# Moving the state-space scan from VectorE to GpSimd in a hybrid layer, with a masked bias table and new room around the scan units

## The chip, the cores and the metric

The kernel runs on one core of a Trainium2 chip. The metric is the device time of one execution in microseconds (us); the kernel before takes 2429.09 us, the median of three runs between 2426.07 and 2430.97. In the profile PE is TensorE (matmul), PEld its weight loads, DVE is VectorE, ACT is ScalarE, POOL is GpSimd, and SP is SyncE, whose queue issues all DMAs of this kernel; SPq, PEq and so on are the sequencers that hand work to the engines.

## The reference

One layer of a streaming encoder over 2048 frames of 1024 features, in float32. One input projection feeds two groups of heads side by side; their outputs are normalised, joined and projected, and a gated feed-forward block follows.

```python
h = rmsnorm(x, norm_mix_g)
u, q, k, v = split(h @ w_in)                      # 512 columns each
# group A: state-space layer, 32 groups of 16 channels, 64 complex states each
lam_bar = exp(lam * dt)
b_bar = (lam_bar - 1) / lam * b
states[t] = lam_bar * states[t - 1] + b_bar @ u[t]
y = gelu(Re(c @ states) + d * u)
y_ssm = y * sigmoid(y @ w_glu + b_glu)
# group B: 8 heads of 64; a chunk of 64 frames attends to itself and the 8 chunks before it
scores = q @ k.T / 8 + bias[head, clip(rel, -128, 128)]   # outside the band: -1e30
y_att = softmax(scores) @ v
x = x + concat(rmsnorm(y_ssm), rmsnorm(y_att)) @ w_out
h2 = rmsnorm(x, norm_ffn_g)
x = x + (silu(h2 @ w_gate) * (h2 @ w_up)) @ w_down
return rmsnorm(x, norm_final_g)
```

## The kernel before

Every matmul operand is held as a high part, rounded for the matmul, and a low part, the rest; a product is three matmuls (`mm3`: high by high, high by low, low by high). High parts are copies on ACT, and the low part is one subtraction, `lo = x - hi`, on DVE or POOL.

**The stages.** From 0 to about 138 us the kernel projects `u`, the input of the state-space layer, in four blocks of 512 columns (`prep`, `group`, `finish`, lines 406 to 482). For each block, `prep` loads eight tiles `xt` (L417), copies their high parts (L419) and subtracts their low parts on DVE (L420); `group` runs 24 matmuls for each of four output tiles. Beside this, `ssm_prologue` builds the powers of `lam_bar` and the small matrices of the state-space layer on DVE (the generator `pro` is advanced between the blocks). Its largest part multiplies six products of 128x576 four times over (tiles `cm` and `v`, lines 273 to 280); these `v` are stored to a DRAM table `vs`. Then come the first transposed, normalised activations `hT`, and the first query, key and value projections; 128 attention steps follow, from 193 to about 832 us; then the gate of the state-space output and the output projection, the gate and up projections (to about 1950 us), and the down projection.

**The attention stage.** `att_phase` emits 128 steps. A step computes the scores of 128 queries of one head against 640 keys (`sc`), adds the bias tile `nb` and takes the minimum on DVE (L736), takes the exponential on ACT (L739), transposes (`pt`, then `pth` on ACT and `ptl` on DVE, L754 and L755), and after four steps multiplies by the values (`pj<-pth,v`). `units` are generators that add work between these parts: the projections of the next 512 frames, and the eight units of the state-space layer. Each `Unit` is advanced by a share of its yields at every step; the matmuls are kept in program order on PE, so the place of a yield fixes what stands in front of what. A state-space unit has `SSM_N` = 42 yields over 15 steps.

**One state-space unit** (`ssm_unit`, lines 486 to 571) serves four of the 32 groups. It loads `U` (8 DMAs), `Bst`, `Tm` and `Vm`, waits `YL` yields, projects with `pj<-U,Bst` (L508; ACT copies the result to `X`, L511), scans, copies the states in four DMAs to `XG` (L557, which also changes their layout), waits `YX` yields, and forms the output with `pj<-U,Tm` and `pj<-XG,Vm` (L565, L566); ACT copies it and eight DMAs store `y` (L570). All tiles of a unit come from a pool with one buffer for each name, and the output tile of a unit bears the name `X` as well. So the next unit's `U` can be loaded only when this unit's output matmuls have read theirs, and its `X` can be written only when the stores of `y` are done.

**The scan.** Along the 256 time blocks it works in groups of eight, with four instructions a step (`step`, lines 525 to 528: multiply, multiply by the swapped part, add, add): 7 steps on 128x128 elements, 7 on 128x16, 3 on 128x4. Two rounds of `carry` (L536, L537) then spread the ends: 8 instructions on 128x42 and 8 on 128x434. The 128 elements of a step stand every eighth in a row of `X`, so 32 bytes apart. In the kernel before these 84 instructions of each unit run on DVE.

**The bias tile.** At the first of a head's four steps `nb` is loaded from the DRAM table `nbs` (L715), and two memsets on POOL write 1e30 into its corners (L716, L717). The low parts of the activations (L640) and of the query, key and value weights (in `split`, L151) are on POOL, but for half of those of the first 512 frames. The split weights are stored to `wss` right behind their split (L613).

The line numbers of helpers stand for many callers: L74 is every matmul, L150 and L151 are the two parts of `split`.

Of the kernel before, what the change touches and what calls it, by code (L numbers as in the profile page):

```python
# [13 lines left out]
ALU = mybir.AluOpType  # L14
AX = mybir.AxisListType

P = 128
# [6 lines left out]
NC = SEQ // L  # L24
GB, GP = 4, 2
H, HD = 8, 64
SB = 512
NSB = SEQ // SB
# [23 lines left out]
CUTL = -8, -2, 2, 7, 13, 19, 23  # L52
ORDER = "sptf"
PINA = True
YL = 8
YX = 9
X1B = 6
TAIL = (0, 512), (512, 256), (768, 256)
MAGIC = 12582912.0
# [32 lines left out]
def f32(ap):  # L92
    return ap.bitcast(F32)
# [297 lines left out]
def u_phase(k, ident, S):  # L391

    tc, nc, io = k.tc, k.nc, k.io
    with ExitStack() as cx:
# [78 lines left out]
        for b in range(1, 4):  # L473
            prep(b)
            next(pro)
            now = [group(b, 0)]
            finish(b - 1, held)
            now += [group(b, 1), group(b, 2)]
            sums(b)
            held = now + [group(b, 3)]  # L480
# [5 lines left out]
def ssm_unit(k, p, psum, S, b, eng):  # L486

    nc = k.nc
# [60 lines left out]
    yield from carry(Xe[:, :, :, 1:, :7], Xe[:, :, :, :3, 7], 8, 3)  # L549
    yield from carry(Xk[:, :, :, 1:, :7], Xk[:, :, :, : NC // 8 - 1, 7], 0, NC // 8 - 1)  # L550

    XG = k.t(p, "XG", [P, GB, NC])
    XGv = XG[:].rearrange("p (q g) c -> p q g c", g=2)
    nc.gpsimd.memset(XG[:, :, 0:1], 0.0)
    for g2 in range(2):
        for c in range(2):
            nc.sync.dma_start(XGv[c * NS : (c + 1) * NS, :, g2, 1:], X[g2 * NS : (g2 + 1) * NS, c, :, : NC - 1])  # L557
# [13 lines left out]
        yield  # L571


SSM_N = YL + GP + 7 + 7 + 3 + 4 + YX + GP


class Unit:
# [21 lines left out]
def att_phase(k, ident, S, pro):  # L599
    tc, nc, io = k.tc, k.nc, k.io  # L600
    with ExitStack() as cx:
        aw = tc.alloc_tile_pool(name="aw", reuse_waits="tile", bufs=1, side="right")
        pfs = cx.enter_context(tc.tile_pool(name="apf", bufs=2, space=bass.MemoryType.PSUM, reuse_waits="tile"))
        hT, vts, qk = {}, {}, {}

        def load_w(sb, n):

            w = k.t(aw, "w", [P, 2, 1024], F32R, bufs=WB)
            if sb == 0:
                raw = k.t(aw, "raw", [P, 1024], bufs=2)  # L610
                nc.sync.dma_start(raw[:], io["w_qk"][n] if n < 8 else io["w_v"][n - 8])
                split(k, w[:, 0], w[:, 1], raw[:], k.wlo_eng)
                nc.sync.dma_start(S["ws"][n], f32(w[:]))  # L613
            else:
                nc.sync.dma_start(f32(w[:]), S["ws"][n])
            return w[:, 0], w[:, 1]

        def hT_unit(sb, q0=0, q1=KT):
            hi, lo = hT.setdefault(sb, ([], []))
            ts = slice(sb * SB, (sb + 1) * SB)  # L620
            xts = {}

            def load(q):
                if q < q1:
                    x = f"{('hi', 'lo')[q % 2]}{q // 2}x" if sb == 0 and q < 2 * DB else None
                    xts[q] = k.t(aw, x, [P, SB]) if x else k.t(aw, "xt", [P, SB], bufs=XB)
                    nc.sync.dma_start(xts[q][:], io["xt"][q * P : (q + 1) * P, ts])

            ahead = 2 if sb else KT
            for q in range(q0, q0 + ahead):  # L630
                load(q)
            for q in range(q0, q1):
                yield
                load(q + ahead)
                xt = xts[q]
                for v, n in zip(hT[sb], ("hi", "lo")):
                    v.append(k.t(aw, f"{n}{q}x" if q < DB and sb % 2 else f"{n}{q}", [P, SB], F32R))
                nc.vector.scalar_tensor_tensor(xt[:], xt[:], k.gm[:, q : q + 1], S["rsn"][:, ts], op0=ALU.mult, op1=ALU.mult)
                nc.scalar.copy(hi[q][:], xt[:])  # L639
                (nc.gpsimd if sb or q % 2 else nc.vector).tensor_tensor(lo[q][:], xt[:], f32(hi[q][:]), op=ALU.subtract)  # L640
            yield

        def qk_unit(sb, pr):
# [11 lines left out]
            for c in range(2):  # L655
                ps = k.t(pfs, "pf", [P, 512])
                wh, wl = ws[c]
                for q in range(KT):
                    cs = slice(q * P, (q + 1) * P)
                    mm3(k.ta, ps[:], wh[:, cs], wl[:, cs], hi[q][:], lo[q][:], q == 0, q == KT - 1)  # L660
                    if q < KT - 1:
                        yield
                for hh in range(2):
# [17 lines left out]
        def v_unit(sb, fh):  # L681
# [5 lines left out]
            for i in range(4):  # L687
                ps = k.t(pfs, "pf", [P, 256])
                ic = slice(i * P, (i + 1) * P)
                for q in range(KT):  # L690
# [4 lines left out]
                    k.ta.matmul(ps[:], lo[q][:, ic], wh, start=False, stop=q == KT - 1)  # L695
                    if q % 2 and q < KT - 1:
                        yield
                vt = vts[4 * sb + i, fh]
                pv3 = ps[:].rearrange("p (h d) -> p h d", h=4)
                nc.scalar.copy(vt[:, :, :HD], pv3)  # L700
# [5 lines left out]
        class Head:  # L706
            pass

        def scores(st):
            sb, pr, hh, qp = st  # L710
            h = 2 * pr + hh
            if qp == 0:
                hd = st_head[sb, h] = Head()
                hd.nb = k.t(aa, "nb", [P, 640], bufs=2)
                nc.sync.dma_start(hd.nb[:], bass.AP(S["nb"].tensor, S["nb"].offset + h * 768 + 1, [[1, P], [1, 640]]))  # L715
                nc.gpsimd.memset(hd.nb[0:64, 0:64], 1e30)  # L716
# [769 lines left out]
def block_kernel(tc, io, phases="pusamf"):  # L1486
    nc = tc.nc
    k = K(tc, io)
    k.ssm_eng, k.wlo_eng = nc.vector, nc.gpsimd
    with ExitStack() as cx:  # L1490
        dram = cx.enter_context(tc.tile_pool(name="dram", bufs=1, space=bass.MemoryType.DRAM))
        cp = cx.enter_context(tc.tile_pool(name="const", bufs=1))
# [2 lines left out]
        def pp():  # L1495
# [2 lines left out]
        S = {  # L1498
            "u": k.t(dram, "u", [DS, L, NC]), "y": k.t(dram, "y", [DS, L, NC]),
            "ya": k.t(dram, "ya_s", [NSB, DS, SB]), "x1": k.t(dram, "x1", [D, SEQ]),  # L1500
            "k": k.t(dram, "ks", [2, H, P, SB]), "nb": k.t(dram, "nbs", [H, 768]),
            "bst": k.t(dram, "bsts", [4, P, 8 * P]), "v": k.t(dram, "vs", [NPR, 2, 2, NS, 9 * CH]),
            "hc": k.t(dram, "hc", [2, 7, P, 4, 512]), "h": k.t(dram, "hs", [4, P, HALF]), "ws": k.t(dram, "wss", [12, P, 2, 1024]),
            "hq": k.t(dram, "hq", [2, F2, 7, P, 512]), "wc": k.t(dram, "wc", [F2, 7, P, 512]), "wt": k.t(dram, "wt", [4, P, HALF]),
# [81 lines left out]
```

## Time and profile before

| what | value |
|---|---|
| median of 3 runs | 2429.09 us |
| the profiled execution, its own time | 2425.27 us |
| its span in the profile | 2423.5 us |
| mean granted clock of TensorE | 0.964 |
| PE busy in the span | 92% |
| DVE, ACT, POOL busy | 69%, 41%, 38% |

The profiled execution's own time is 1.8 us above its span; the rest lies around it. Busy shares are means over stages with different limits, so the stages are read apart. "Idle before, releaser" tells how long an engine stood before a group of instructions and what ended that.

### The profile page before, as it was taken

The numbers are of one execution on the slowest core, as the hardware profiler recorded it, in microseconds if no ns is written. First come the engines' busy times: TensorE is split into PE (matmuls) and PEld (weight loads), VectorE is DVE, ScalarE is ACT, GpSimd is POOL, SyncE is SP. The second block draws the span as 40 slices with busy tenths as digits, with TensorE's granted clock in tenths as the row PEclk, the third lists the DMA queues.
The fourth block names the chain that finished last, engine by engine and source line by source line (L and its number), as shares of the span: only waits on it lengthen the run. The fifth ranks groups of instructions, "written<-read, shape, count | busy, mean of one in ns | idle before, by whom it ended". The sixth has DMA issues, their size and how long they took to land.

```text
span 2423.5 us, 30933 instructions
## 1 busy us (share of the span) xinstructions
PE 2224.6 (92%) x10744; PEld 1862.5 (77%) x10744; DVE 1665.3 (69%) x2943; ACT 1000.3 (41%) x1671; POOL 909.0 (38%) x613
## 2 busy tenths in 40 slices
PE   6876878899998799999999999899999989999996
PEld 5655767788787678877888888688888868888886
DVE  8965688777878675656676666867655456569676
ACT  4233544455544754234333334433333343345322
POOL 4321210010100043257555555755555554445542
PEclk8887999999999999999999999999999989999998
DMA  5655676566554353564455455645433277555551
GB/s 159 174 194 203 216 206 199 174 192 191 169 176 123 121 170 122 183 229 149 135 183 177 158 187 206 237 170 202 154 122 95 71 295 253 190 200 200 182 191 70
DMA packets 223132, 425.75 MB, mean 176 GB/s; under 512 B 30384, under 2 KB 70832, under 8 KB 215872
## 3 DMA queue, kind: packets, MB, share of 16 engines
q1 hardware_dynamic: 222976, 423.79, 53.6%
q8 instruction: 84, 1.38, 0.2%
q14 instruction: 72, 0.59, 0.1%
HBM read 283.97 MB, written 129.26 MB: 171 GB/s over the span
## 4 chain that ended last, share of the span: by engine, by line
PE 56%; DVE 2%; DMA 2%; POOL 1%; issue 1%; ACT 1%; SPq 0%; DVEq 0%; POOLq 0%; ACTq 0%
PE X L74 18%; PE ps L74 18%; PE Y L74 9%; PE big L74 6%; PE W L74 5%; DMA lo<-hc 1%; DVE lo L151 1%; POOL c L151 0%; POOL lo L151 0%; POOL sa L1005 0%; DMA hd<-wc 0%; POOL sa L1004 0%; DVE acc L1451 0%; DVE S L1253 0%; DVE g L1318 0%
## 5 line engine op out<-in xcount | busy, mean ns | idle before, releaser
L74 PE MATMUL X<-hi,c 128*128 128x512 f32 x1408 | 451.2, 391 | 7.9 <-POOL c L151 3.2
L74 PE MATMUL ps<-hd,hd 128*128 128x512 f32 (+1 forms) x1968 | 434.7, 383 | 8.0 <-DVE hd L151 4.6
L74 PEld LDWEIGHTS ps<-hd,hd 128*128 128x128 f32 x1968 | 361.3, 191 | 80.1 <-DVE hd L151 4.9
L151 POOL TENSOR_TENSOR c<-S,c 128x512 fp32r<-128x512 f32 x176 | 251.8, 1432 | 243.8 <-ACT c L150 239.8
L74 PEld LDWEIGHTS X<-hi,c 128*128 128x128 f32 x1408 | 265.1, 188 | 65.5 <-ACT u L1271 4.0
L74 PE MATMUL X<-lo,c 128*128 128x512 f32 x704 | 274.9, 390 | 0.0
L151 POOL TENSOR_TENSOR hd<-hd 128x1536 fp32r<-128x1536 f32 (+1 forms) x53 | 190.3, 3596 | 208.7 <-ACT hd L150 185.5
L150 ACT CAST hd<-hd 128x1536 fp32r<-128x1536 f32 (+1 forms) x106 | 147.4, 1392 | 227.1 <-DMA hd<-hq 155.3
L151 POOL TENSOR_TENSOR c<-raw,c 128x512 fp32r<-128x512 f32 x132 | 189.6, 1436 | 130.6 <-ACT c L150 105.5
L74 PE MATMUL Y<-hi,c 128*128 128x512 f32 x704 | 227.2, 393 | 11.3 <-DVE u L1275 11.3
L1399 DVE TENSOR_TENSOR acc<-acc,ps 128x512 f32<-128x512 f32 x196 | 129.2, 682 | 87.0 <-PE ps L74 84.4
L74 PE MATMUL pf<-hi,w 128*128 128x512 f32 x416 | 157.7, 428 | 10.5 <-ACT hi L639 10.5
L74 PEld LDWEIGHTS Y<-hi,c 128*128 128x128 f32 x704 | 133.5, 190 | 41.0 <-DVE u L1275 13.0
L74 PE MATMUL big<-m,woh 128*128 128x512 f32 x512 | 163.7, 402 | 0.2 <-DVE yr L941 0.2
L150 ACT CAST c<-S 128x512 fp32r<-128x512 f32 x176 | 109.3, 621 | 114.6 <-PE Y L74 57.8
L74 PEld LDWEIGHTS X<-lo,c 128*128 128x128 f32 x704 | 132.7, 188 | 27.3
L716 POOL MEMSET nb<- 64x64 f32 x32 | 4.6, 144 | 387.9 <-DMA nb<-nbs 246.0
L1271 ACT COPY u<-X 128x512 f32<-128x512 f32 x132 | 76.9, 584 | 176.4 <-PE X L74 176.4
L739 ACT ACTIVATE s<-s,mn 128x640 f32<-128x640 f32 (+4 forms) x128 | 97.9, 765 | 121.4 <-DVE mn L736 102.9
L150 ACT CAST c<-raw 128x512 fp32r<-128x512 f32 x132 | 82.1, 622 | 149.7 <-PE Y L74 82.3
L736 DVE CUSTOM_DVE_ANT_0 s<-sc,nb 128x640 f32<-128x640 f32 (+4 forms) x128 | 94.1, 735 | 70.5 <-PE sc L74 56.6
L151 DVE TENSOR_TENSOR hd<-hd 128x1536 fp32r<-128x1536 f32 (+1 forms) x53 | 113.4, 2141 | 35.7 <-ACT hd L150 35.6
(370 smaller groups left out, 4812.2 us busy)
## 6 DMA issues: line engine op xcount, KB each, us to landing
w<-wss SPq DMA_DIRECT2D x36, 1024.0 KB, 5.5
hq<-g SPq DMA_DIRECT2D x140, 256.0 KB, 2.1
hd<-hq SPq DMA_DIRECT2D x42, 768.0 KB, 4.5
hd<-wc SPq DMA_DIRECT2D x42, 768.0 KB, 6.0
raw<-in_w_gate SPq DMA_DIRECT2D x44, 512.0 KB, 3.8
raw<-in_w_up SPq DMA_DIRECT2D x44, 512.0 KB, 4.2
wc<-px SPq DMA_DIRECT2D x66, 256.0 KB, 2.9
wss<-w SPq DMA_DIRECT2D x12, 1024.0 KB, 4.4
```

Of the source, the lines that this page charges most:

```text
L74: return self.tc.keep_in_program_order(self.tc.nc.tensor.matmul(*a, **b))
L150: nc.scalar.copy(hi, raw)
L151: (lo_eng or nc.gpsimd).tensor_tensor(lo, raw, f32(hi), op=ALU.subtract)
L716: nc.gpsimd.memset(hd.nb[0:64, 0:64], 1e30)
L736: nc.vector.tensor_tensor_reduce(s[:, :nk].rearrange("p (a b) -> p a b", a=nch), ps[:, :nch, :half], hd.nb[:, nk - 1 :: -1].rearrange("p ( ...
L739: nc.scalar.activation(s[:, :nk], s[:, :nk], AF.Exp, bias=mn[:], scale=-1.0, accum_out=sums[sb, pr][:, hh, qp : qp + 1])
L1271: nc.scalar.copy(u[:], ps[:])
L1399: V.tensor_tensor(a, a, ps[:], op=ALU.add)
```

## The change

The state-space scan goes to POOL (`k.ssm_eng`). The low parts of the attention weights, and of all activations but half of the first 512 frames', go to DVE (`k.wlo_eng`, and the choice at L640). A unit now waits 4 yields instead of 8 between its loads and its projection, 6 new yields stand between the end of the scan and the transfers to `XG`, and 7 instead of 9 behind those; the sum stays 42. `XG` is allocated once and its first column cleared once. The bias tiles with their corners are built once in a DRAM table `nbms`, with one DMA that expands 8x768 entries into 1024 rows of 640 (2.6 MB) and two that write the corners from a memset tile; a head's tile is loaded two steps before the head begins, and nothing is written into it. The stores of the split weights move behind the first matmuls that use them.

```diff
-YL = 8
-YX = 9
+YL = 4
+YW = 6
+YX = 7
...
         for b in range(1, 4):
             prep(b)
             next(pro)
+            if b == 2:
+                corner = k.t(p1, "corner", [64, H, 64])
+                nc.gpsimd.memset(corner[:], 1e30)
+                nc.sync.dma_start(S["nbm"][:], bass.AP(S["nb"].tensor, S["nb"].offset + 1, [[768, H], [1, P], [1, 640]]))
+                for m in range(2):
+                    nc.sync.dma_start(S["nbm"][:, m * 64 : m * 64 + 64, m * 576 : m * 576 + 64].rearrange("h p c -> p h c"), corner[:])
...
-    XG = k.t(p, "XG", [P, GB, NC])
+    if b == 0:
+        k.XG = k.t(p, "XG", [P, GB, NC])
+        nc.gpsimd.memset(k.XG[:, :, 0:1], 0.0)
+    XG = k.XG
     XGv = XG[:].rearrange("p (q g) c -> p q g c", g=2)
-    nc.gpsimd.memset(XG[:, :, 0:1], 0.0)
+    for _ in range(YW):
+        yield
...
                 split(k, w[:, 0], w[:, 1], raw[:], k.wlo_eng)
-                nc.sync.dma_start(S["ws"][n], f32(w[:]))
+                keep[n] = w
...
+        def keep_w(n):
+            if n in keep:
+                nc.sync.dma_start(S["ws"][n], f32(keep.pop(n)[:]))
...
-                (nc.gpsimd if sb or q % 2 else nc.vector).tensor_tensor(lo[q][:], xt[:], f32(hi[q][:]), op=ALU.subtract)
+                (nc.vector if sb or q % 2 == 0 else nc.gpsimd).tensor_tensor(lo[q][:], xt[:], f32(hi[q][:]), op=ALU.subtract)
...
+                    if q == 2:
+                        keep_w(4 * c + pr)
...
+                if i == 0:
+                    for r in range(2):
+                        keep_w(8 + 2 * r + fh)
...
+        def load_nb(h):
+            nb = k.t(aa, "nb", [P, 640], bufs=2)
+            nc.sync.dma_start(nb[:], S["nbm"][h])
+            return nb
...
-                hd.nb = k.t(aa, "nb", [P, 640], bufs=2)
-                nc.sync.dma_start(hd.nb[:], bass.AP(S["nb"].tensor, S["nb"].offset + h * 768 + 1, [[1, P], [1, 640]]))
-                nc.gpsimd.memset(hd.nb[0:64, 0:64], 1e30)
-                nc.gpsimd.memset(hd.nb[64:128, 576:640], 1e30)
+                hd.nb = nbs.pop(h) if nbs else load_nb(h)
...
+            if qp == 2 and (sb, h) < (NSB - 1, H - 1):
+                nbs[(h + 1) % H] = load_nb((h + 1) % H)
...
-    k.ssm_eng, k.wlo_eng = nc.vector, nc.gpsimd
+    k.ssm_eng, k.wlo_eng = nc.gpsimd, nc.vector
```

The order in which the instructions stand on an engine is set by the program and by a scheduler, and the change moves rows at two places that the prediction speaks of.

**SP in the projection of `u`, second block.** The rows run from the fourth `xt` of the block on. Before, `kts` is a table of the state-space layer, and the other four `xt` follow at once:

```order
L417 DMA xt_782<-in_xp 128x512
L363 DMA kts_79<-kt_1331 16x8x128
L417 DMA xt_791<-in_xp 128x512
L417 DMA xt_800<-in_xp 128x512
L417 DMA xt_809<-in_xp 128x512
```

Now the same place reads as below; `nbms` is the expansion of the bias table, `bbs` and `vs` are stores of what DVE has computed in the prologue (a second store of the same `bbs` pair and the rest of the first `vs` pair are left out at the lines of dots):

```order
L418 DMA xt_783<-in_xp 128x512
L480 DMA nbms_69<-nbs_70 1024x1x640
L344 DMA bbs_79<-bbr_563 64x16x16
L344 DMA bbs_79<-bbi_564 64x16x16
...
L352 DMA vs_72<-v_236_702 64x4x144
L352 DMA vs_72<-v_237_703 64x4x144
...
L352 DMA vs_72<-v_242_718 64x4x144
L352 DMA vs_72<-v_243_719 64x4x144
...
L418 DMA xt_792<-in_xp 128x512
L418 DMA xt_801<-in_xp 128x512
```

The last four `xt` loads of the block stand behind four stores of `bbs` and eight of `vs`.

**DVE at the same place.** These are the rows around the fifth and sixth low part of that block (`lo<-xt_791`, `lo<-xt_800`). Before, they stand among the powers of `lam_bar` (`pr`, `pi`):

```order
L282 TENSOR_TENSOR bbi_563<-cm_193_569,cm_194_570 128x256
L420 TENSOR_TENSOR lo_270_794<-xt_791,hi_269_793 128x512
L273 TENSOR_TENSOR cm_197_580<-pr_574 128x16
L274 TENSOR_TENSOR cm_198_581<-pi_575 128x16
L420 TENSOR_TENSOR lo_274_803<-xt_800,hi_273_802 128x512
L275 TENSOR_TENSOR pr_574<-cm_197_580,cm_198_581 128x16
```

Now they stand behind all powers and behind 23 of the 24 multiplications of 128x576 that form `v`:

```order
L279 TENSOR_TENSOR cm_340_1059<-pi_576,ci_340 128x576
L276 TENSOR_TENSOR v_337_1056<-cm_339_1058,cm_340_1059 128x576
L278 TENSOR_TENSOR cm_341_1063<-pr_575,ci_340 128x576
L279 TENSOR_TENSOR cm_342_1064<-pi_576,cr_339 128x576
L421 TENSOR_TENSOR lo_271_795<-xt_792,hi_270_794 128x512
L421 TENSOR_TENSOR lo_275_804<-xt_801,hi_274_803 128x512
L281 SCALAR_TENSOR_TENSOR v_338_1057<-cm_341_1063,cm_342_1064 128x576
```

What moved is the second half of the block's low parts: 160 rows of DVE stood ahead of them, now 253 do.

**PE between two state-space units.** Behind the first unit's output the rows are the same up to the last `pf<-w,lo` below; `sc`, `pj<-ident,rb` and `pt` belong to the attention step that follows, `pf<-hi,w` to the next projection. Before:

```order
L74 MATMUL pf_2702<-w_2431,lo_467_1593 128x256
L74 MATMUL sc_2796<-k_593_2217,q2h_2215 128x512
L74 MATMUL sc_2796<-k_593_2217,q2l_2216 128x512
L74 MATMUL pj_2803<-ident_80,rb_2758 128x128 x4
L77 MATMUL pt_2810<-ident_80,s_2681 128x128 x2
L74 MATMUL pf_2823<-hi_452_1557,w_2715 128x512
```

Now:

```order
L75 MATMUL pf_2698<-w_2456,lo_469_1597 128x256
L75 MATMUL pj_2793<-U_2721,Bst_2730 128x256 x2
L75 MATMUL pj_2800<-U_2721,Bst_2730 128x256 x2
L75 MATMUL sc_2813<-k_604_2243,q2h_2241 128x512
L75 MATMUL sc_2813<-k_604_2243,q2l_2242 128x512
L75 MATMUL pj_2820<-ident_81,rb_2754 128x128 x4
```

The projection `pj<-U,Bst` of the next unit stands sixteen rows sooner behind the output of the unit before it; the output matmuls of the units have kept their places.

More of the change, by code (lines that the diff above doesn't have):

```diff
@@ L571, in ssm_unit @@
         yield
-SSM_N = YL + GP + 7 + 7 + 3 + 4 + YX + GP
+SSM_N = YL + GP + 7 + 7 + 3 + 4 + YW + YX + GP
 class Unit:
@@ L603, in att_phase @@
         pfs = cx.enter_context(tc.tile_pool(name="apf", bufs=2, space=bass.MemoryType.PSUM, reuse_waits="tile"))
-        hT, vts, qk = {}, {}, {}
+        hT, vts, qk, keep = {}, {}, {}, {}
         def load_w(sb, n):
@@ L707, in att_phase @@
             pass
+        nbs = {}
+        def load_nb(h):
+            nb = k.t(aa, "nb", [P, 640], bufs=2)
+            nc.sync.dma_start(nb[:], S["nbm"][h])
+            return nb
         def scores(st):
@@ L1500, in block_kernel @@
             "ya": k.t(dram, "ya_s", [NSB, DS, SB]), "x1": k.t(dram, "x1", [D, SEQ]),
-            "k": k.t(dram, "ks", [2, H, P, SB]), "nb": k.t(dram, "nbs", [H, 768]),
+            "k": k.t(dram, "ks", [2, H, P, SB]), "nbm": k.t(dram, "nbms", [H, P, 640]), "nb": k.t(dram, "nbs", [H, 768]),
             "bst": k.t(dram, "bsts", [4, P, 8 * P]), "v": k.t(dram, "vs", [NPR, 2, 2, NS, 9 * CH]),
```

## The prediction

> **What bounds the kernel now.** I read the page first, then the windows of 60 us, then the waits of the attention stage, then the two ends of a state-space unit in the timeline.
>
> ```profile
> PE 2224.6 (92%) x10744; PEld 1862.5 (77%) x10744; DVE 1665.3 (69%) x2943; ACT 1000.3 (41%) x1671; POOL 909.0 (38%) x613
> PE   6876878899998799999999999899999989999996
> DVE  8965688777878675656676666867655456569676
> 0.00:60.00 60.00, 40.78 (x154) 32.00 (x155) 50.61 (x191) 28.12 (x48) 24.84 (x22) 0.86 0.59 159
> 60.00:120.00 60.00, 48.72 (x205) 39.29 (x204) 59.52 (x131) 15.96 (x28) 19.31 (x14) 0.89 0.61 173
> 360.00:420.00 60.00, 51.79 (x303) 44.53 (x304) 49.30 (x141) 28.98 (x59) 0.58 (x4) 1.00 0.63 184
> 213.45:795.20 581.75, 504.96 (x2994) 443.40 (x2993) 449.55 (x1219) 292.13 (x618) 55.66 (x97) 0.96 0.61 184
> ```
>
> The columns of a window are its length, the busy time of PE, PEld, DVE, ACT and POOL, and the granted clock. PE is nearly full from about 800 us on, and the change leaves the order of PE there alone: what is won or lost comes from the first 800 us. Of those, 60 to 120 us belong to DVE (59.52 of 60). In the attention stage PE leads but isn't full, and POOL is almost idle (0.58 of 60).
>
> ```profile
> DVE s L736 <- PE sc L74: 56.6, 31, 7.7
> PE pt L77 <- DVE ptl L755: 33.0, 32, 2.3
> PE sc L74 <- DVE mn L736: 23.2, 9, 10.5
> PE pj L74 <- DMA Tm<-kts: 11.2, 4, 3.7
> POOL nb L716 <- DMA nb<-nbs: 246.0, 21, 25.5
> ```
>
> These rows give the time waited in all, the times, and the longest. PE waits for DVE (33.0 and 23.2 us) where the scan delays `ptl` and `mn`, and four times for the loads of a unit (11.2). POOL's 246.0 us only show an idle engine.
>
> ```profile
> L74 PE MATMUL pj<-U,Bst x64: 377/379/634, 213.5 to 741.8; 128*128 128x256 f32 x64
> L74 PE MATMUL pj<-XG,Vm x64: 378/379/379, 275.1 to 795.2; 128*128 128x256 f32 x64
> 257.22 0.63 PE L74 MATMUL pf<-lo,w 128*128 128x512 f32 x1
> 257.65 1.05 PE L74 MATMUL pf<-hi,w 128*128 128x512 f32 x2
> 261.30 0.39 PE L74 MATMUL pf<-lo,w 128*128 128x512 f32 x1
> 261.53 0.62 PE L74 MATMUL pf<-hi,w 128*128 128x512 f32 x2
> ```
>
> The eight units reach from 213.45 (first `U,Bst`) to 795.2 (last `XG,Vm`): 582 us. A 128x512 matmul takes 0.23 us from start to start at full clock (261.30 to 261.53). With every form counted at its closest spacing, read in the same way (0.118 for 256 columns, 0.147 for a score of 320, 0.108 for a transpose, 0.216 for one of a unit's own), the PE work in these 582 us is 470 us, so **112 us are lost**; the window agrees, with 77 idle and a clock of 0.96. Behind a pause PE is slower for some 4 us (257.22 to 257.65: 0.43 a matmul), so a pause costs about 1.9 us more.
>
> **The scan's price on POOL.** First what it costs DVE, then POOL's rows.
>
> ```profile
> L525 DVE TENSOR_TENSOR st<-X,a x136: 163/182/2255, 217.6 to 770.5; 128x128 f32<-128x128 f32 x56, 128x16 f32<-128x16 f32 x56, 128x4 f32<-128x4 f32 x24
> L536 DVE TENSOR_TENSOR fx<-X,a x64: 153/596/2691, 239.1 to 781.2; 128x42 f32<-128x42 f32 x32, 128x434 f32<-128x434 f32 x32
> L525 DVE TENSOR_TENSOR st<-X,a 128x128 f32<-128x128 f32 (+2 forms) x136 | 40.9, 301 | 11.2 <-ACT X L511 8.0
> L537 DVE TENSOR_TENSOR X<-X,fx 128x42 f32<-128x42 f32 (+1 forms) x64 | 29.9, 468 | 1.0
> L1434 POOL TENSOR_TENSOR sb<-sb,sg x6: 724/736/746, 2387.4 to 2407.1; 128x256 f32<-128x256 f32 x6
> L151 POOL TENSOR_TENSOR c<-S,c x176: 1283/1292/1842, 1093.9 to 1937.1; 128x512 fp32r<-128x512 f32 x176
> 59.36 4.07 POOL L425 TENSOR_TENSOR acc<-acc,sq 128x512 f32<-128x512 f32 x3 [7.92 <-ACT sq L423]
> L527 DVE TENSOR_TENSOR X<-X,st 128x128 f32<-128x128 f32 x56 | 22.5, 402 | 0.0
> L755 DVE TENSOR_TENSOR ptl<-pt,pth 128x128 fp32r<-128x128 f32 x36 | 10.3, 286 | 2.8 <-ACT pth L754 2.4
> ```
>
> The six scan lines together take 214.5 us of DVE, 26.8 a unit. On POOL, 256 elements take 0.736 us and 512 take 1.292: 2.17 ns an element and 0.18 us an instruction. Instructions that depend on each other start 1.39 us apart (4.07 less 1.29, halved): 0.09 more. A unit is then 28 x 0.55 (128 elements) + 28 x 0.305 (16) + 12 x 0.28 (4) + 8 x 0.36 (42) + 8 x 1.21 (434) = **40 us** if layout costs nothing. But the step operands lie 32 bytes apart, and no POOL row has that. On DVE the same 128 elements take 402 ns so spread and 286 packed, 1.4 times. The bounds are 40 and, with each element at twice the price everywhere, 57 us. I take an element of a step at 1.5 times, 44 us, and 1 us for contention: **45 us**, near the DVE ratio.
>
> The Trainium skill, "GPSIMD Engine Reference", section 7, says that a read with a step above 8 bytes costs about 2.9 cycles an element instead of 1.9 on GpSimd; by that rule the unit is an estimated 44 us as well, without contention. Its section 4.1 tells one not to put elementwise work on GpSimd, about twice slower with two inputs, which speaks against the change; here POOL's 40 to 45 against DVE's 26.8 agrees, and whether that time is hidden decides.
>
> **What the scan hides behind.** From `U,Bst` to the output of its unit a chain runs: 2.3 us until the last copy to `X`, the scan, 4.3 us for the four issues to `XG` and their landing: 2.3 + 45 + 4.3 = 51.6 us. Beside it PE has, by the matmuls that stand between the two groups in the changed kernel's order, priced as above, 37, 40, 51, 49, 51, 49, 55 and 45 us of work in the eight units. PE would wait 14.6, 11.6, 0.6, 2.6, 0.6, 2.6, 0 and 6.6: **39 us**. The first two units are the poor ones.
>
> **The hand-over between units.** `YL` 4 puts `U,Bst` sooner behind the last output.
>
> ```profile
> 431.40 5.51 SPq L570 DMA_DIRECT2D y<-X  x8
> 436.95 3.23 SPq L492 DMA_DIRECT2D U<-u  x7
> 442.24 1.97 PE L74 MATMUL pj<-U,Bst 128*128 128x256 f32 x8 [2.35 <-DMA Tm<-kts]
> ```
>
> The output ended at 430.6; the copy, eight stores and seven loads in a row on SP, and a landing give 11.7 us to the next `U,Bst`, and PE already waited 2.35. PE work in that gap is now 5.9, 7.7, 5.8, 10.4, 9.0, 5.8 and 6.2 us, so it waits 5.8, 4.0, 5.9, 1.3, 2.7, 5.9 and 5.5: **31 us**, where the four waits of before sum to 11.2. Queued behind it on PE are the next scores, and DVE and ACT wait for those.
>
> **The rest of the stage.** The scan leaves `ptl` and `mn` alone; stretches of four steps without a scan lose 0.3 us, so I leave 8 us for such losses and for slow matmuls behind a pause that no later wait hides. Elapsed: 470 + 39 + 31 + 8 = 548 instead of 582: **-34 us**. The low parts on DVE (24 of 0.68 us for activations, 12 of 128x1024) are far less than the scan it gives up, and cost nothing as long as DVE stays below PE; if DVE were full they would cost some 30 us.
>
> ```profile
> L1318 DVE TENSOR_TENSOR g<-g,u x66: 691/1232/1786, 1130.3 to 1952.4; 128x512 f32<-128x512 f32 x66
> L1318 DVE TENSOR_TENSOR g<-g,X x22: 671/676/686, 1147.1 to 1954.7; 128x512 f32<-128x512 f32 x22
> ```
>
> While POOL works, a DVE instruction with two operands in SBUF takes 1232 (the median of `g<-g,u`), and the one that reads PSUM stays at 676. `s`, `ptl`, `k` and `q2l` read PSUM, so the scan on POOL won't slow them. The Trainium skill, "SBUF — State Buffer", section "SBUF: two separate sides", calls it an exclusive lock held for the whole instruction, and these rows agree.
>
> **The start.** The bias expansion brings a reorder. In the second block of `u` four `xt` loads stand behind eight stores of `vs` on SP, and their low parts behind 93 more rows on DVE.
>
> ```profile
> 49.55 0.80 PE L74 MATMUL ps<-lo,wuh 128*128 128x512 f32 x1 [3.81 <-DVE lo L420]
> L277 DVE TENSOR_TENSOR cm<-pr,ci 128x576 f32<-128x576 f32 x4 | 4.1, 1022 | 0.1
> L280 DVE SCALAR_TENSOR_TENSOR v<-cm,cm 128x576 f32<-128x576 f32 x4 | 3.0, 755 | 0.0
> L74 PE MATMUL ps<-hi,wuh 128*128 128x512 f32 x91 | 38.7, 425 | 5.6 <-DVE us L447 5.6
> ```
>
> PE resumes the block at 49.55 now. Of the 93 rows 23 are products of 128x576, two of six lines at 1.02 and four at 0.755, 19 us; the other 70 are small, some 9 us. PE then resumes near 77.5. From there it has 275 matmuls (91 or 92 of each of three kinds) of 0.23, 63 us, and some 10 us of waits and small matmuls, so the stage ends at 150.5 instead of 137.7: **+13 us**. DVE has done the products by then, so PE leads; were DVE still behind, it would be +17. The bounds are 0, if the loads arrive in time, and +17.
>
> ```profile
> 148.10 0.42 SPq L627 DMA_DIRECT2D hi0x<-in_xt  x1
> 151.78 2.67 SPq L613 DMA_DIRECT2D wss<-w  x2
> 154.51 0.46 SPq L627 DMA_DIRECT2D lo0x<-in_xt  x1
> ```
>
> SP stood from 148.5 to 151.78 before the two `wss` stores, and spent 2.67 us on them, with seven `hT` loads behind. Both go: -6. In the new order the raw value weights stand behind the first stores of `k`, which wait for PE; I take 4 us for that, between 0 and the 6 just won. Net of the start: **+11 us** (-2 to +17). The bias tile costs nothing: its load comes two steps ahead, and POOL has room.
>
> **Sum.** 2425.3 (the profiled execution's own time) - 34 + 11 = 2402. That execution is 3.8 us under the median, so I say **2405 us**. PE's order behind 800 us is the same, and I count it at nothing there.
>
> **Rivals.**
> *POOL is slower than I think (47 us or more, chance 0.32).* The more units wait, the nearer each us of scan comes to 8 us in all. With 48 us the waits for the scan are 60 us, and the 13 left of the attention stage's gain meet the 11 lost at the start: no change. At 50 us they are 76 and the time is 2443; at 52 us 92, and 2459; at 57 us 132, and 2499. The place is `pj<-XG,Vm` behind a transfer that waits for `X`, and SP stands still there, with every load behind it. For it: 84 instructions in a chain, with operands of four dimensions, on an engine whose rows are all packed. Against it: nothing but the DVE ratio. This is the one that ends slower.
>
> *The scan is cheaper (0.18).* At 40 us a unit the chain is 46.6, and only the first two and the last unit wait, 18 us: 2384.
>
> *The reorder at the start isn't on the path (0.1).* If the loads behind the `vs` stores are early enough, or the later blocks make the delay good since DVE has its products behind it, the 13 us are not lost: 2392. Against it: PE already stands at 49.55 for a low part of that block.
>
> **How the numbers follow.** My forecast has a chance of 0.4. The range takes in the cheap scan with half of the start's loss on the one side, and a scan of 51.5 us on the other: 2378 to 2455; the worst of the slow scans lie above it, at about 0.12. A measurement of this kernel can tell about 0.2% (5 us) from no change. Of the slow scans 0.05 fall within that, and 0.03 of the forecast: 0.08 the same, 0.27 slower, and 0.4 + 0.18 + 0.1 - 0.03 = 0.65 faster.
>
> **What would show it.** The form rows of the scan on POOL: near 0.6 us for 128 elements, 45 us a unit. PE's rows `pj<-XG,Vm` with an idle time of about 15 us at the first unit and near none at the third to seventh. `pj<-U,Bst` idle by 4 to 6 us at most hand-overs, with the loads of `U` as releaser. PE's pause in the second block of `u` until about 77 us, and the first `s<-sc,nb` near 204 instead of 193.1. Waits of `pt` for `ptl` near nothing. What would make it wrong first is the scan's time: above 48 us a unit the gain is gone.

## The result and the profile after

The changed kernel takes 2542.65 us (median of 4 runs, 2536.94 to 2547.71) against 2429.24 before: a ratio of 1.0468, with a 95% interval from 1.0441 to 1.0494. It is **113 us slower**. The forecast was 2405, and the range ended at 2455. The profiled execution has a span of 2545.9 us, 122.4 longer than before.

The row of the scores `s` tells where the attention stage begins and ends; its columns are the shortest, median and longest duration in ns, and the first and last start. The first row is the kernel before, the second the changed one.

```profile
L736 DVE CUSTOM_DVE_ANT_0 s<-sc,nb x128: 280/815/851, 193.1 to 830.9; 128x640 f32<-128x640 f32 x96, 128x128 f32<-128x128 f32 x8, 128x256 f32<-128x256 f32 x8, 128x384 f32<-128x384 f32 x8
```

```profile
L762 DVE CUSTOM_DVE_ANT_0 s<-sc,nb x128: 274/824/826, 214.9 to 947.3; 128x640 f32<-128x640 f32 x96, 128x128 f32<-128x128 f32 x8, 128x256 f32<-128x256 f32 x8, 128x384 f32<-128x384 f32 x8
```

The start is 21.8 us longer, the attention stage 94.6 (732.4 instead of 637.8), and the rest 6.0 (in the runs below the rest varies by as much). So the loss has two places, both ahead of 950 us.

These are the windows of the attention stage, before and after: the length, the busy time of PE, PEld, DVE, ACT and POOL, the granted clock, and the DMA's share and GB/s.

```profile
193.10:830.90 637.80, 547.01 (x3234) 480.65 (x3235) 472.90 (x1278) 324.10 (x668) 62.16 (x103) 0.96 0.60 181
```

```profile
214.90:947.30 732.40, 567.54 (x3257) 503.56 (x3258) 325.65 (x640) 322.96 (x669) 269.01 (x673) 0.87 0.53 161
```

PE stands 164.9 us of the stage instead of 90.8, and is busy 20.5 us longer, at a granted clock of 0.87 instead of 0.96. So 74 of the 94.6 us are waits of PE, and some 20 are slower matmuls.

This is the row of busy times on the changed kernel's page.

```profile
PE 2245.0 (88%) x10744; PEld 1885.6 (74%) x10744; DVE 1505.1 (59%) x2307; ACT 999.4 (39%) x1671; POOL 1109.6 (44%) x1179
```

DVE is relieved as meant (1505 us instead of 1665), and POOL stood 391.6 us waiting for a scan to begin (the row of L532 further down): it isn't overloaded. But POOL is now 12% of the page's chain that ended last. The waits of the attention stage, SP's own queue among them, tell why; these are the rows of after that answer to those of before.

```profile
SPq L568 <- POOL X L544: 181.2, 16, 25.3
PE pt L78 <- DVE ptl L781: 39.2, 9, 15.5
PE pf L75 <- DMA w<-wss: 24.2, 2, 12.6
PE sc L75 <- DMA q2h<-q2h: 20.5, 2, 19.5
PE pf L75 <- ACT hi L654: 19.5, 2, 13.7
PE pj L75 <- DMA Tm<-kts: 18.7, 5, 7.1
DVE xt L653 <- DMA xt<-in_xt: 48.5, 8, 23.1
DVE ya L805 <- DMA ya_s<-ya: 36.0, 2, 18.2
```

SP, which issues every DMA, stands 181.2 us at the transfers to `XG` (L568), waiting for POOL's last carry. Before, the same wait was 19.1 us. And PE waits for things that SP loads: weights from `wss`, copies of `q2h`, the next `hi` (which come from `xt` loads). None of them has to do with the scan. They stand behind it on SP. Even 31 of the 39.2 us for `ptl`, two waits of 15, are of this kind: there DVE stands for `ya_s<-ya`, a store of an attention output that SP issues behind the transfers, and `ptl` is behind that on DVE. The prediction had these waits near nothing.

One unit shows it, the fourth. First SP, PE and POOL of the changed kernel; a row is the start, the duration, the instruction and its count, and in brackets the idle time ahead of it.

```profile
480.45 3.48 PE L75 MATMUL pj<-U,Bst 128*128 128x256 f32 x8 [4.16 <-DMA Tm<-kts]
485.58 0.51 POOL L532 TENSOR_TENSOR st<-X,a 128x128 f32<-128x128 f32 x1 [42.95 <-ACT X L518]
495.54 0.48 SPq L733 DMA_DIRECT2D nb<-nbms  x1
517.98 6.47 SPq L568 DMA_DIRECT2D XG<-X  x4
521.40 1.03 POOL L544 TENSOR_TENSOR X<-X,fx 128x434 f32<-128x434 f32 x1
524.54 0.54 SPq L626 DMA_DIRECT2D w<-wss  x1
525.18 0.48 SPq L687 DMA_DIRECT2D q2h<-q2h  x1
528.32 1.19 SPq L642 DMA_DIRECT2D xt<-in_xt  x2
532.18 0.61 PE L75 MATMUL sc<-k,q2h 128*128 128x320 f32 x1 [19.54 <-DMA q2h<-q2h]
```

SP reaches the transfers at 496.0, 15.6 us after the projection began. The scan, which began at 485.58, lets the first of the four go at 517.98, and the other three at 522.46, when its last instruction has ended. For 22 us SP issues nothing, then for 4 more one transfer alone; then weights, `q2h` and `xt` follow in a row, and PE has stood 19.54 us for `q2h` when it goes on at 532.18. In the kernel before SP reached the transfers of this unit at 483.3, 41 us after the projection, and 3.4 us later they went:

```profile
482.37 0.89 SPq L627 DMA_DIRECT2D xt<-in_xt  x2
486.67 1.29 SPq L557 DMA_DIRECT2D XG<-X  x2
```

It is so in every unit. Read in the same way, SP reaches the transfers of the eight units 31, 27, 20, 16, 10, 12, 12 and 16 us after the projection began, and the first goes after 36 to 41. In the kernel before SP came there after 53 us in the first unit, falling to 30 in the last. So the change has also moved the transfers forward on SP, against the six yields that now stand ahead of them in the program. With the scan on DVE again (e3 below) they stand at 32 to 43 us. Why the order of SP goes with the engine of the scan, no run shows.

### The profile page after: what moved, and what is told of

It reads as the page before. It is cut to its first block, busy times and chain, and to the rows that moved or that the text cites. A ratio compares the mean times of both kernels' runs of the same rounds, so it can differ in the third digit from the quotient of the medians.

```text
span 2545.9 us, 30843 instructions
## 1 busy us (share of the span) xinstructions
PE 2245.0 (88%) x10744; PEld 1885.6 (74%) x10744; DVE 1505.1 (59%) x2307; ACT 999.4 (39%) x1671; POOL 1109.6 (44%) x1179
## 4 chain that ended last, share of the span: by engine, by line
PE 61%; issue 13%; POOL 12%; DVE 7%; DMA 4%; ACT 2%; SPq 1%; DVEq 0%; POOLq 0%; ACTq 0%
PE ps L75 18%; PE X L75 18%; PE Y L75 9%; PE big L75 7%; PE W L75 4%; PE pf L75 3%; POOL X L535 2%; POOL X L534 2%; POOL X L544 2%; POOL fx L543 2%; POOL st L532 2%; POOL st L533 2%; PE pj L75 1%; DMA lo<-hc 1%; DVE lo L421 1%
## 5 line engine op out<-in xcount | busy, mean ns | idle before, releaser
L532 POOL TENSOR_TENSOR st<-X,a 128x128 f32<-128x128 f32 (+2 forms) x136 | 46.2, 340 | 401.7 <-ACT X L518 391.6
L1425 DVE TENSOR_TENSOR acc<-acc,ps 128x512 f32<-128x512 f32 x196 | 129.3, 681 | 90.8 <-PE ps L75 90.6
L75 PEld LDWEIGHTS Y<-hi,c 128*128 128x128 f32 x704 | 134.2, 191 | 43.7 <-DVE u L1301 15.6
L780 ACT CAST pth<-pt 128x640 fp32r<-128x640 f32 (+3 forms) x152 | 83.6, 550 | 153.8 <-PE pt L78 149.8
L75 PE MATMUL Y<-lo,c 128*128 128x512 f32 x352 | 138.7, 394 | 0.0
```

The lines of the kernel that those rows point to most:

```text
L75: return self.tc.keep_in_program_order(self.tc.nc.tensor.matmul(*a, **b))
L532: eng.tensor_tensor(t[:, :, :, :n], src, ar, op=ALU.mult)
L780: nc.scalar.copy(pth[:, a:b, qp, :], pt[:, a:b, :])
L1425: V.tensor_tensor(a, a, ps[:], op=ALU.add)
```

## The experiments

Theory A: the transfers to `XG` stand too early on SP for a scan on POOL, and everything behind them is late. Rival B: the chain of a unit (projection, scan, output, hand-over) is too long. For the start: the expansion of the bias table moves the loads of `u`, against other parts of the change.

Each kernel was run beside the kernel before on one chip. "Attention" is the last start of `s` less the first, from the same row as above.

| kernel | median us | ratio to before, interval | first `s` | attention |
|---|---|---|---|---|
| before | 2429.24 | 1 | 193.1 | 637.8 |
| changed | 2542.65 | 1.0468 [1.0441, 1.0494] | 214.9 | 732.4 |
| e1_pin | 2498.78 | 1.0284 [1.0265, 1.0303] | 212.8 | 689.3 |
| e2_table_first | 2525.95 | 1.0395 [1.0375, 1.0415] | 200.9 | 729.5 |
| e3_scan_dve | 2463.67 | 1.0143 [1.0125, 1.0161] | 208.3 | 659.4 |
| e4_xg_pool_queue | 2431.15 | 1.0003 [0.9992, 1.0015] | 211.7 | 622.4 |
| e5_queue_table_late | 2414.86 | 0.9939 [0.992, 0.9958] | 200.9 | 618.2 |
| e6_yl8 | 2393.41 | 0.9845 [0.9825, 0.9865] | 202.8 | 598.0 |
| e7_y_pool_queue | 2400.57 | 0.9879 [0.9858, 0.9899] | 200.4 | 596.0 |
| e8_before_queue | 2432.15 | 1.0002 [0.9987, 1.0017] | 191.8 | 641.3 |
| e9_all | 2393.86 | 0.9847 [0.9831, 0.9862] | 200.4 | 591.2 |
| e10_scan_dve | 2432.36 | 1.0003 [0.9991, 1.0015] | 201.2 | 631.4 |
| e11_before_yl4 | 2469.42 | 1.0154 [1.0133, 1.0176] | 191.9 | 674.2 |
| e12_no_table | 2386.26 | 0.9814 [0.9798, 0.983] | 187.3 | 604.7 |

### The queue: e1 and e4

e1 changes the issue order alone (`k.nbl` is the last bias load):

```diff
-            nc.sync.dma_start(nb[:], S["nbm"][h])
+            k.nbl = nc.sync.dma_start(nb[:], S["nbm"][h])
...
-    for g2 in range(2):
-        for c in range(2):
-            nc.sync.dma_start(XGv[c * NS : (c + 1) * NS, :, g2, 1:], X[g2 * NS : (g2 + 1) * NS, c, :, : NC - 1])
+    with k.tc.issue_after(k.nbl.ins):
+        for g2 in range(2):
+            for c in range(2):
+                nc.sync.dma_start(XGv[c * NS : (c + 1) * NS, :, g2, 1:], X[g2 * NS : (g2 + 1) * NS, c, :, : NC - 1])
```

> The changed kernel, with the four transfers to XG queued on SP behind the bias-tile load of the step in which the program has them, so some four steps later than they now stand there; nothing else moves. Theory A (the transfers stand too soon on SP, wait there for the scan, and hold the loads of weights and activations behind them): SP's wait for POOL at these transfers falls from 181 us to below 60, the attention stage shortens by 50 to 80 us of the 95 that it lost, and the time is 2465 to 2495. Rival B (the chain projection, scan, output is itself too long, with the scan on POOL and the hand-over of 4 yields): the scan ends no sooner, so the time stays at 2530 to 2550.

e4 changes the queue alone:

```diff
-            nc.sync.dma_start(XGv[c * NS : (c + 1) * NS, :, g2, 1:], X[g2 * NS : (g2 + 1) * NS, c, :, : NC - 1])
+            nc.gpsimd.dma_start(XGv[c * NS : (c + 1) * NS, :, g2, 1:], X[g2 * NS : (g2 + 1) * NS, c, :, : NC - 1])
```

> The changed kernel with the four transfers to XG issued from POOL's own queue instead of SP's, right behind the scan that they wait for. Theory A (SP's queue is what holds the loads): SP waits for no scan any more, the attention stage shortens by 60 to 90 us, and the time is 2455 to 2485. Rival B (the chain of scan and output): unchanged within 10 us, or longer by the issue on POOL.

SP's wait in e1, then PE's waits in e4 (in which SP's list has no wait for the scan any more):

```profile
SPq L569 <- POOL X L544: 111.4, 16, 18.4
```

```profile
PE pj L75 <- DMA Tm<-kts: 29.1, 7, 7.1
PE pt L78 <- DVE ptl L781: 11.2, 9, 2.1
```

e1 falls short of its numbers: SP's wait is 111.4 us and not below 60, and the time is 4 us above the range. SP still comes to the transfers 18 to 32 us after the projections, ahead of the scan's end. But what SP waits less, 70 us, shortens the stage by 43. With the queue of POOL SP stops waiting, and the stage is 110 us shorter, more than theory A had written. That is all of the 94.6 us and 15 more: e4 is as fast as the kernel before, with the loss of the start still in it. The scan takes no less time in e4 (37 to 43 us a unit, against 36 to 40), so rival B falls as the cause of the loss.

### The scan's engine: e3, e10 and e8

```diff
-    k.ssm_eng, k.wlo_eng = nc.gpsimd, nc.vector
+    k.ssm_eng, k.wlo_eng = nc.vector, nc.vector
```

e3 makes this edit in the changed kernel, e10 in e6, where `XG` goes by POOL's queue.

> The changed kernel with the scan back on DVE and all else as changed. Theory A (what was lost in the attention stage comes with the scan on POOL, because the transfers to XG then stand sooner on SP than the scan allows): the transfers stand later again, SP waits at most 25 us for the scan, and the attention stage is within 20 us of the 639 of before; with the start's loss left in, 2440 to 2470. Rival (the loss comes from the 4 yields at the hand-over, the low parts on DVE or the new bias loads): above 2500.

> The kernel of e6 with the scan back on DVE; the transfers to XG stay on POOL's queue. Theory (taking the scan off DVE is worth what the prediction counted, DVE no longer delaying ptl and mn): PE's waits for ptl come back from 10 us to 30 or more, and the time is 25 to 40 us above e6, 2418 to 2433. Rival (with the queue in order, the engine of the scan makes no difference, since PE leads either way): within 8 us of e6.

PE's wait for `ptl` in e10, and the same row in e6:

```profile
PE pt L78 <- DVE ptl L781: 35.2, 33, 2.4
```

```profile
PE pt L78 <- DVE ptl L781: 10.1, 8, 2.1
```

Both times came as theory A had them (e3's stage, 659.4 us, is 0.4 over what it allowed). With SP's queue as changed, the scan on POOL costs 79 us (2542.65 against 2463.67); with the transfers out of SP's way, 8 yields and the late table it gains 39 (2432.36 against 2393.41). The same edit has both signs. The rows show most of the gain: of the 33 us by which the stage is shorter, 25 are PE's waits for `ptl`.

e8 puts the transfers of the kernel before on POOL's queue, with the edit of e4.

> The kernel before with nothing changed but the transfers to XG issued from POOL's queue. Theory (in the kernel before SP hardly stands for the scan, 19 us in all, so the queue matters only with the scan on POOL): 2420 to 2434. Rival (SP is short of room in any case, and most of e4's 111 us come from unloading it): below 2400.

The interval takes in no change. The queue is worth 111 us in the changed kernel, with the scan on POOL, and nothing in the kernel before, with the scan on DVE, so it is no gain of its own.

### The hand-over: e6, e11 and e7

e6 is e5 (below) with other numbers of yields; e11 is the kernel before with the changed kernel's `YL`:

```diff
-YL = 4
-YW = 6
+YL = 8
+YW = 2
```

```diff
-YL = 8
-YX = 9
+YL = 4
+YX = 13
```

> The kernel of e5 with 8 yields between the loads of a unit and its projection instead of 4, and 2 instead of 6 behind the scan. Prediction's own sum for the hand-over: PE's waits for U fall from 29 us to about 11, the scan's chain loses as much room but binds only in the first two units and the last, +8: 8 to 12 us less than e5. Rival (PE's waits for U are made good later, or the chain of the scan takes all of it back): within 4 us of e5, or longer.

> The kernel before with 4 instead of 8 yields between a unit's loads and its projection, and 13 instead of 9 behind the scan, so that the output keeps its place. Prediction's sum for the hand-over: PE's waits for U rise from 11 to about 31 us, 2445 to 2455. Rival (the waits are made good at the units' outputs): within 6 us of the kernel before.

PE's waits for a unit's loads in e5, in e6 and in e11:

```profile
PE pj L75 <- DMA Tm<-kts: 28.9, 7, 6.9
```

```profile
PE pj L75 <- DMA Tm<-kts: 7.1, 3, 3.7
PE pj L75 <- DMA XG<-X: 4.2, 2, 2.5
```

```profile
PE pj L74 <- DMA Tm<-kts: 33.6, 7, 7.9
```

The prediction's 31 us for the hand-over at `YL` 4 is met (28.9 and 33.6); at 8 it is 7.1 where 11 was expected. e6 gains 21 us where 8 to 12 were expected: the waits for `U` fall by 22 and not by 18, and the scan's chain takes little back, since PE waits only 4.2 us for `XG`. e11 loses 38 us where some 20 were expected, for 22 us more of these waits. Its stage is 36 us longer, and its window shows how: PE stands 26 us more (116.8 instead of 90.8) and is busy 10 us longer (557.4 instead of 547.0), at a granted clock of 0.93 instead of 0.96. So in e11 a wait cost more than its own length.

e7 moves the stores of `y` to POOL's queue in e5:

```diff
-                nc.sync.dma_start(S["y"][b * F : (b + 1) * F, j, :].rearrange("(g c) t -> c g t", c=CH), Y[j * CH : (j + 1) * CH])
+                nc.gpsimd.dma_start(S["y"][b * F : (b + 1) * F, j, :].rearrange("(g c) t -> c g t", c=CH), Y[j * CH : (j + 1) * CH])
```

> The kernel of e5 with the eight stores of y issued from POOL's queue too, so that the loads of the next unit's U don't stand behind them on SP. Theory (the hand-over is the row of issues on SP, 11.7 us, of which the stores are about 4): waits for U fall from 29 us to below 12, time 15 to 20 us below e5. Rival (stores on POOL are slower to issue, 1.5 us each as for XG, and the next X waits for them): no gain, or slower than e5.

```profile
PE pj L75 <- DMA Tm<-kts: 10.8, 3, 5.1
```

The wait for `U` falls from 28.9 to 10.8 us, as expected, and the time by 14 (15 to 20 expected): the hand-over is a row of issues on SP.

### The start: e2, e5, e9 and e12

e2 writes the table ahead of the first block of `u`; e5 (e4's queue with it) behind the last store of `u` (`k.ul`; `issue_after` fixes only the order of issue):

```diff
         pro = ssm_prologue(k, ident, S)
+        corner = k.t(p1, "corner", [64, H, 64])
+        nc.gpsimd.memset(corner[:], 1e30)
+        nc.sync.dma_start(S["nbm"][:], bass.AP(S["nb"].tensor, S["nb"].offset + 1, [[768, H], [1, P], [1, 640]]))
...
         prep(0, first)
```

```diff
         finish(3, held)
+        corner = k.t(p1, "corner", [64, H, 64])
+        nc.gpsimd.memset(corner[:], 1e30)
+        with tc.issue_after(k.ul.ins):
+            nc.sync.dma_start(S["nbm"][:], bass.AP(S["nb"].tensor, S["nb"].offset + 1, [[768, H], [1, P], [1, 640]]))
...
```

> The changed kernel, with the masked bias table built ahead of the first block of the u projection instead of ahead of the second; the scan and the attention stage as changed. Theory A (the place of the expansion moves the loads of the second block behind the prologue's products): the first scores come at 193 to 198 us instead of 214.9, and the time falls by 17 to 22 us to 2520 to 2526. Rival (the later weight stores, the corner writes or the 2.6 MB themselves cost the start): at most 8 us come back, 2535 or more.

> The kernel of e4 (transfers to XG from POOL's queue), with the masked table written behind the last store of u, so that DVE's rows in the u projection stand as before the change. Theory A for the start (the place of the expansion is all of it): first scores at 190 to 198 us instead of 211.7, attention 623 us as in e4, time 2408 to 2418, about 0.6% below the kernel before. Rival (something else in the change, the delayed weight stores or the low parts on DVE, costs the start): first scores at 203 or later, 2420 or more.

In the changed kernel PE stands for the loads of the second block, then for their low part, and later for DVE once more (the first three rows); SP issues the four `xt` behind eight stores of `vs`:

```profile
72.53 0.80 PE L75 MATMUL ps<-hi,wuh 128*128 128x512 f32 x1 [30.35 <-ACT hi L420]
77.26 0.80 PE L75 MATMUL ps<-lo,wuh 128*128 128x512 f32 x1 [3.94 <-DVE lo L421]
116.36 2.04 PE L75 MATMUL pp<-ident,no 128*128 128x128 f32 x8 [8.38 <-DVE no L109]
59.51 8.66 SPq L352 DMA_DIRECT2D vs<-v  x8
68.27 2.02 SPq L418 DMA_DIRECT2D xt<-in_xp  x4
```

Both kernels bring the first scores to 200.9, so 11 to 14 us of the 21.8 are the place of the table. Both fall short of what was expected of the first scores (193 to 198 for e2, 190 to 198 for e5), though both times are within their ranges. In e2 the stage of `u` itself ends some 10 us later than before the change (its last matmuls start at 146.9 instead of 137.2). In e5 that stage ends as before; there SP stands 9.1 us for the landing of the expansion before it can write the corners, with the `hT` loads behind:

```profile
146.71 0.75 SPq L487 DMA_DIRECT2D nbms<-nbs  x1
162.30 1.28 SPq L489 DMA_DIRECT2D nbms<-corner  x2
165.29 0.42 SPq L642 DMA_DIRECT2D hi0x<-in_xt  x1
172.22 0.80 PE L75 MATMUL pf<-hi,w 128*128 128x512 f32 x1 [22.46 <-ACT hi L654]
```

e9 puts the corners behind the last of the `hT` loads (`k.xl`), with the edit of e7; e12 leaves the table out of e6:

```diff
+        with tc.issue_after(k.xl.ins):
+            for m in range(2):
+                nc.sync.dma_start(S["nbm"][:, m * 64 : m * 64 + 64, m * 576 : m * 576 + 64].rearrange("h p c -> p h c"), corner[:].unsqueeze(1).to_broadcast([64, H, 64]))
```

```diff
-            nc.sync.dma_start(nb[:], S["nbm"][h])
+            nc.sync.dma_start(nb[:], bass.AP(S["nb"].tensor, S["nb"].offset + h * 768 + 1, [[1, P], [1, 640]]))
...
                 hd.nb = nbs.pop(h) if nbs else load_nb(h)
+                nc.vector.memset(hd.nb[0:64, 0:64], 1e30)
+                nc.vector.memset(hd.nb[64:128, 576:640], 1e30)
```

> e6 (XG from POOL's queue, table behind the last store of u, 8 yields at the hand-over), with the stores of y on POOL's queue as in e7, and the corner writes behind the hT loads on SP instead of ahead of them. Theory (in e6 SP stands until the expansion has landed, with the hT loads behind the corner writes, 8 us; and 7 us of waits for U are left): first scores at 193 to 197 us, waits for U below 3 us, time 2376 to 2386. Rival (the expansion's own traffic costs the start, and the rest of the hand-over is made good elsewhere): 2389 or more.

> The kernel of e6 without the masked table: the bias tile is loaded two steps ahead from the small table as it is, and two memsets on DVE write its corners at the head's first step. Theory (what is left of the start's loss in e5, e6 and e9, 7 to 10 us, is the expansion of 2.6 MB, whose traffic and landing the hT loads wait for): first scores at 190 to 196 us instead of 202.8, time 2382 to 2389. Rival (the delayed weight stores and the low parts on DVE cost that time, or the 64 memsets on DVE hold the scores up): within 4 us of e6's 2393, or longer.

e9 is a miss: 2393.86 where 2376 to 2386 were expected, no better than e6. PE's waits for `U` are down to 1.2 us, as expected, but the first scores stay at 200.4, and PE still stands 14.71 us for the first `hi`:

```profile
148.61 5.30 SPq L638 DMA_DIRECT2D hi0x<-in_xt  x1
165.77 0.79 PE L75 MATMUL pf<-hi,w 128*128 128x512 f32 x1 [14.71 <-ACT hi L650]
```

So it isn't the corner writes alone. Without the table the first scores come at 187.3, sooner than the 190 to 196 expected, 15.5 us sooner than in e6 and 5.8 sooner than before the change. Its `hT` row of PE:

```profile
154.34 0.79 PE L75 MATMUL pf<-hi,w 128*128 128x512 f32 x1 [3.28 <-ACT hi L648]
```

The expansion itself costs the start wherever it was put. The traces of e9 and e12 show two ways, of about 5 us each. In e9 SP stands 5.2 us behind the expansion, so its second `hT` load goes out at 153.96 instead of 148.59. And the loads land later: `hi1x` and `lo1x` after 10.9 and 10.7 us, against 6.0 and 6.2 in e12. That the second is the expansion's traffic is likely, but no run shows it. The attention stage of e12 is 6.7 us longer than e6's, so the net is 7 us. e12, 2386 us, is the best kernel of the study: 1.9% below the kernel before (ratio 0.9814, interval 0.9798 to 0.983).

## Why the prediction was wrong

**The scan's price: too high, and not what decided.** The prediction put a scan on POOL at 45 us a unit, between 40 and 57. From its first instruction to the end of its last it took 36 to 40, in the mean 37 (485.58 to 522.43 in the fourth unit), which is 1.4 times DVE's 26.8. The forms in the changed kernel:

```profile
L532 POOL TENSOR_TENSOR st<-X,a 128x128 f32<-128x128 f32 x56 | 27.7, 495 | 395.4 <-ACT X L518 391.6
L534 POOL TENSOR_TENSOR X<-X,st 128x128 f32<-128x128 f32 x56 | 31.6, 564 | 0.0
L543 POOL TENSOR_TENSOR fx<-X,a 128x434 f32<-128x434 f32 x32 | 34.6, 1083 | 2.5
```

The packed fit of the prediction gives 0.46 us for 128 elements and 1.12 for 434. The strided steps take 0.49 to 0.56, and the 434 elements 1.07 to 1.08. The factor of 1.5 on an element was too much, and so were the 0.09 us at every instruction: only some of them pay it, as the last section shows. The Trainium skill's rule on strided reads ("GPSIMD Engine Reference", section 7) would make the element's part half as long again, some 0.60 us an instruction, an estimate; these rows are below that.

**The step that failed: what the scan hides behind.** The sum let PE work 37 to 55 us beside the chain, up to the output `pj<-XG,Vm`, and took that as the room of the scan. The room ended much earlier: at the point where SP reaches the transfers, 15.6 us after the projection in the fourth unit. SP doesn't pass over an instruction that waits. The first rival named the place ("SP stands still there, with every load behind it") and still priced it by the output, with a threshold of 48 us a unit. At 37 us it came true, at a price of 95 us in the attention stage. The order of SP around the transfers was to be read like that of PE, and wasn't. The output itself hardly waited: PE's list of waits in the changed kernel has no row for `XG`.

**The second step that failed: the 8 us left for all other losses.** What was forecast of DVE came, once SP is out of the way: PE's waits for `ptl` fall from 33.0 us to 11.2 in e4. The hand-over is met as well (29.1 for 31), and the 39 us of waits for the scan did not come at all (PE waits 0.3 us for `XG`). By the sum's own terms e4, the POOL scan and `YL` 4 with another queue, would have gained more than the 34 us forecast. Its attention stage is 622.4 instead of 637.8, only 15 less. This is its window from the first projection to the last output, 18 us below the 581.75 in the prediction:

```profile
235.20:798.70 563.50, 505.23 (x3009) 451.35 (x3008) 305.73 (x579) 291.30 (x620) 290.90 (x704) 0.95 0.64 191
```

Take away the 470 us of work and the 29 of the hand-over, and 64 us are left, where the sum had 8. PE is busy for 505 us, as in the kernel before (504.96), which is 35 above the 470; the other 29 are small waits. The sum let nearly all of this go with the scan, and it stayed.

**The start: right in its cause, half its size.** PE had the first high part at 72.53 and went on behind the first low part at 77.26, where 77.5 was forecast, for the reason given. But the stage of `u` was to end 73 us later, for "DVE has done the products by then, so PE leads". It took 84, not much less than the 88 before the change: DVE was still busy (58.08 of the 60 us from 60 to 120), PE stood again until 116.36 for `no`, and the clock was 0.73 in that window. So of a delay of 28 us the stage made good 4, and not 15.

```profile
60.00:120.00 60.00, 34.42 (x137) 27.17 (x138) 58.08 (x78) 20.48 (x36) 23.01 (x15) 0.73 0.54 146
```

Net, 21.8 us instead of 11; the bound given was 17. The sum gave the expansion of the table no time of its own; e12 beside e6 shows 15 us of it in the start.

**The rivals.** The cheap scan came true (37 us, below its 40) without its gain. The start was on the path. The slower side had the right place, SP, and the wrong price.

## What to carry to other kernels

When work moves to a slower engine, look at the queue that hands on its result, not only at the engine that uses it: an in-order queue ends the room of the slow work where it reaches the first transfer that waits, and what stands behind has nothing to do with it. A transfer that waits long for an engine can be issued from that engine's own queue, where only work of the same engine stands behind it: that one word was worth 111 us here, and nothing where the wait was short (e8). A one-time table that saves work later can cost more where it is built, in the start of a kernel where every load is awaited, than it saves: here 15 us against 7.

## What the runs showed of the hardware that was not expected

These rows follow the first of the 28 instructions on 128 elements in the fourth unit of the changed kernel (485.58, 0.51 us); the last is the first behind the 28.

```profile
486.02 0.51 POOL L533 TENSOR_TENSOR st<-X,sw 128x128 f32<-128x128 f32 x1
486.46 0.59 POOL L534 TENSOR_TENSOR X<-X,st 128x128 f32<-128x128 f32 x1
487.13 0.54 POOL L535 TENSOR_TENSOR X<-X,st 128x128 f32<-128x128 f32 x1
487.74 0.49 POOL L532 TENSOR_TENSOR st<-X,a 128x128 f32<-128x128 f32 x1
500.70 0.23 POOL L532 TENSOR_TENSOR st<-X,a 128x16 f32<-128x16 f32 x1
```

L535 needs what L534 wrote, and the next L532 what L535 wrote. There 0.08 and 0.07 us lie between the end of one and the start of the other, close to the prediction's 0.09. L533 doesn't need L532, and L534 (which takes the product of L532) doesn't need L533; each of them begins 0.07 us before the one ahead ends, as the trace dates them. So the 28 follow each other at 0.54 us (15.12 divided by 28), where the prediction put 0.69 with its factor of 1.5. And a step of 32 bytes costs POOL some 15% over packed operands (0.52 us in the mean of the four lines against the fit's 0.46), where DVE took 40% more.

The transfers to `XG` in the changed kernel and in e4 (count, size, median us from issue to landing):

```profile
XG<-X SPq DMA_DIRECT2D x32, 127.5 KB, 2.4
```

```profile
XG<-X POOLq DMA_DIRECT2D x32, 127.5 KB, 4.4
```

From POOL's queue they land 2 us later, and an issue takes POOL 0.6 us (616 ns in the mean of e6's 32), not the 1.5 of e7's rival. e4 is faster all the same, so neither decided anything here.
